# Output weights of layer 1 prepared inside the recurrence, and four operand groups instead of six

## The chip, the cores and the metric

The kernel runs on 1 core of one Trainium2 chip. The metric is the device time of one execution in microseconds (us). Three runs of the kernel before took 3316.65, 3322.71 and 3327.7 us; the median is 3322.71.

## What is computed

A decoder trunk of two residual layers on 2048 tokens of width 1024, in float32. Layer 0 mixes with pooling and convolution, layer 1 with a chunked gated DeltaNet; each is followed by a mixture of experts. Cut to what matters here, layer 1 is:

```python
u = h @ w_in                                   # q, k, v, z and the gates
state, o = scan(step, state0, chunks)          # the delta rule, in order of time
#   v_new = u_i - w_i @ state
#   o_i   = qg_i @ state + a_i @ v_new
#   state = state * d_i + kd_i^T @ v_new
y = (o * rsqrt(mean(o*o) + EPS) * onorm_g * silu(z)) @ w_out
x = x + g_m * y                                # g_m: one gate per output column, from the conditioning c
hn = rmsnorm(x, norm_ffn) * (1 + sc_f) + sh_f
x = x + g_f * hierarchical_moe(hn)             # router logits, top 1 group, top 2 experts
```

## The kernel before, in words

**Stages.** `trunk` runs layer 0, its experts (`moe(0)`), the mixer of layer 1 (`mixer1`: `dn_project`, then `dn_chain`), the output projection with the router (`out_phase(1)`), the experts (`moe(1)`) and a final norm. A tile framework orders each engine's instructions ahead of the run from dependencies, program order as priority, and a cost model; each engine then works through its list in order and waits at semaphores. A tile's space in SBUF is given to a later tile once the earlier one's last reader is done.

**The recurrence (`dn_chain`).** The 2048 tokens are 16 blocks of 128; 8 heads are two groups of four (`hg`). For a block and a group, `R(bl, hg)` has three steps: `dv = VP - KE S` (four matmuls, DVE, L1463), `vt = tt dv` (four matmuls, ACT, L1471), then the output `po = QG S + A vt` (L1476, L1477) and the new state `S = etot*S + KDD vt` (POOL makes `sd` at L1468, DVE adds at L1481). The five operands A, KE, QG, KDD, VP of a group lie in one tile `stin` of 1280 KB, loaded by `load` (L1388). There are six such tiles, in two pools of three. `load_n` (L1395 to L1403) brings the small pieces from which `M(bl, hg)` builds the block's inverse `tt` (POOL spreads at L1356; L1425 to L1452 on PE, DVE and ACT). `M` runs one to two blocks ahead of `R`. `tail` (L1496, L189, L1502, L1507) scales the outputs of the block before, `O` (L1514, L1517) transposes them, `store` (L1523) writes them to the scratch tensor `yT`. All these transfers are issued on SP's queue, in one order. Blocks 0 to 4 also carry `dn_invert(1, 1)`, DVE work on the tile `xblk` (L1321, L1322) whose result (L1323, L1327) `load_n(8)` and later ones read.

**The projection (`out_phase`, l = 1).** Its code begins by loading `w_out1`, eight pieces of 512 KB (L509), into the tiles that the experts use later for their weights (`raw`); then `load_y(0)` and `load_y(1)` (L485, L489: `yr` from `yT`, `zr` from `zT`; L490 multiplies them). Each weight piece is split into a rounded part `woh` (ACT, L237) and a remainder `wol` (DVE, L238); `yr` likewise into `yh`, `yl`. Three rows, `gm` (the gate), `ga` and `sh`, are spread over the partitions by `row_bcast` (PE L199, ACT L200). Then 16 tiles of 128 tokens: `project(t)` does 48 matmuls (L536) into a PSUM tile `po` and the epilogue

```python
nc.vector.tensor_mul(h, ps, gm)        # L540
nc.vector.tensor_add(x, h, x)          # L541
```

followed by the norm (L544, L189, L546, L547); `logits(t - 1)` transposes (L564), multiplies by the router's weights (L571) and, per group of tiles, calls `route`. After the last tile `rank_experts` gives the order of the experts, from which `moe(1)` takes the addresses of its loads.

## Time and profile before

| | us |
|---|---|
| median of three runs | 3322.71 |
| the profiled execution | 3314.97 |
| its span in the trace | 3313.2 |
| PE busy (matmuls) | 2908.4 (88%) |
| DVE busy | 2443.9 (74%) |
| ACT busy | 1495.1 (45%) |
| POOL busy | 1022.7 (31%) |

The span has six stages; times are us from its start. The stages that the change touches are the recurrence (2219 to 2475) and the projection with the router (2475 to 2760). A line such as `2490.76 1.23 DVE L490 TENSOR_TENSOR yr<-yr,zr ... [1.38 <-DMA zr<-zT]` means: begun at 2490.76, 1.23 us long, on DVE, line 490, writes yr from yr and zr, and DVE sat idle for 1.38 us before it until a DMA had brought zr. PEclk is TensorE's granted clock as a share of full speed. Matmul ends are modelled, so the distance between starts is their pace.

### The profile page before, as it was taken

To read this page: it belongs to the slowest core of one execution; us is meant where nothing else is said; L and a number is where in the kernel's file an instruction comes from. 1 tells how busy PE (TensorE), PEld (TensorE's weight loads), DVE (VectorE), ACT (ScalarE), POOL (GpSimd) and SP (SyncE) were. 2 spreads that over 40 slices of the span, in tenths; PEclk is the share of its full clock that TensorE was granted. 3 is DMA by queue.
4 is the path that set the end of the run, shared out by engine and by line. 5 is a ranking of instruction groups with operands and counts; after the bars stand their busy time and mean duration, and the time that the engine had idled before them with its cause. 6 is when DMAs were issued, how large, how long until landed. Compare 5 with 4: busy or idle time off the path is not lost. (4 is left out here: it accounts for less than half of the span.)

```text
span 3313.2 us, 41885 instructions
## 1 busy us (share of the span) xinstructions
PE 2908.4 (88%) x14192; PEld 2313.6 (70%) x14192; DVE 2443.9 (74%) x3805; ACT 1495.1 (45%) x2560; POOL 1022.7 (31%) x877
## 2 busy tenths in 40 slices
PE   4979878787999997999989999988988996999991
PEld 3756666566777774888867877777987765777770
DVE  4998999757878875777876786858445556888783
ACT  6135233216656546443444433444772214666552
POOL 0142323333443431322212131235530212434431
PEclk9989999898999998999999999998999997999996
DMA  6225233638999854545352343457957437989876
GB/s 222 85 73 209 83 132 127 216 121 303 309 281 298 268 169 160 171 153 191 136 174 83 104 144 106 144 148 223 268 195 227 153 121 253 308 279 297 264 232 217
DMA packets 384984, 633.37 MB, mean 191 GB/s; under 512 B 111232, under 2 KB 245504, under 8 KB 384768
## 3 DMA queue, kind: packets, MB, share of 16 engines
q1 hardware_dynamic: 355904, 563.38, 49.9%
q0 software_dynamic: 28864, 67.30, 8.7%
q8 instruction: 113, 1.85, 0.2%
q14 instruction: 103, 0.84, 0.1%
HBM read 484.46 MB, written 175.44 MB: 199 GB/s over the span
## 5 line engine op out<-in xcount | busy, mean ns | idle before, releaser
L260 PE MATMUL pm<-hh,wh 128*128 128x512 f32 x1408 | 565.9, 402 | 0.8 <-ACT wh L237 0.7
L262 PE MATMUL pm<-hh,wl 128*128 128x512 f32 x1408 | 556.5, 396 | 3.6 <-DVE wl L238 3.6
L261 PE MATMUL pm<-hl,wh 128*128 128x512 f32 x1408 | 555.4, 395 | 4.2 <-DVE hl L233 4.2
L238 DVE TENSOR_TENSOR wl<-wr,wh 128x1024 fp32r<-128x1024 f32 x384 | 452.2, 1218 | 40.7 <-ACT wh L237 37.3
L237 ACT ACTIVATE wh<-wr 128x1024 fp32r<-128x1024 f32 x384 | 399.5, 1057 | 134.7 <-PE py L851 56.8
L838 POOL DMA_INDIRECT acc<-ys,ixs x102 | 263.5, 2584 | 435.3 <-DVE wl L238 149.6
L261 PEld LDWEIGHTS pm<-hl,wh 128*128 128x128 f32 x1408 | 269.2, 191 | 63.4 <-DVE hl L233 4.6
L260 PEld LDWEIGHTS pm<-hh,wh 128*128 128x128 f32 x1408 | 269.1, 191 | 62.5 <-issue 4.6
L262 PEld LDWEIGHTS pm<-hh,wl 128*128 128x128 f32 x1408 | 268.6, 191 | 62.9 <-DVE wl L238 5.7
L817 PE MATMUL pu<-wh,xt 128*128 128x512 f32 x656 | 268.8, 410 | 0.5 <-ACT xt L237 0.5
L818 PE MATMUL pu<-wl,xt 128*128 128x512 f32 x656 | 261.3, 398 | 0.0
L819 PE MATMUL pu<-wh,xt 128*128 128x512 f32 x656 | 260.3, 397 | 0.0
L238 DVE TENSOR_TENSOR wl<-wraw,wh 128x1024 fp32r<-128x1024 f32 x88 | 110.9, 1261 | 155.4 <-ACT wh L237 155.2
L286 DVE SCALAR_TENSOR_TENSOR acc<-cin,wfir,acc 128x512 f32<-128x512 f32 (+1 forms) x320 | 214.7, 727 | 0.1
L536 PE MATMUL po<-woh,yh 128*128 128x512 f32 x512 | 172.4, 413 | 30.6 <-ACT yh L237 22.1
L237 ACT ACTIVATE wh<-wraw 128x1024 fp32r<-128x1024 f32 x88 | 93.2, 1059 | 227.4 <-PE pm L261 227.2
L1220 DVE SCALAR_TENSOR_TENSOR dacc<-ub,cols,dacc 128x1024 f32<-128x1024 f32 x144 | 186.8, 1297 | 2.8
L536 PE MATMUL po<-wol,yh 128*128 128x512 f32 x512 | 166.6, 405 | 0.0
L536 PE MATMUL po<-woh,yl 128*128 128x512 f32 x512 | 165.5, 402 | 0.3 <-DVE yl L238 0.3
L795 POOL DMA_INDIRECT xg<-hn,ixs x102 | 112.4, 1102 | 162.6 <-PE tp L805 87.3
L189 POOL TENSOR_TENSOR rs<-rs1t,expo 128x1 f32<-128x1 f32 x48 | 28.3, 589 | 381.1 <-DVE rs1t L187 339.6
L819 PEld LDWEIGHTS pu<-wh,xt 128*128 128x128 f32 x656 | 124.1, 189 | 30.8 <-DVE xt L238 0.5
(377 smaller groups left out, 6362.2 us busy)
## 6 DMA issues: line engine op xcount, KB each, us to landing
wr<-in_w_up_dram SPq DMA_DIRECT2D x256, 512.0 KB, 7.6
wr<-in_w_down_dram SPq DMA_DIRECT2D x128, 512.0 KB, 7.0
modw<-in_modwT_dram SPq DMA_DIRECT2D x96, 512.0 KB, 5.1
wraw<-in_w_in_dram SPq DMA_DIRECT2D x88, 512.0 KB, 3.6
stin<-stg SPq DMA_DIRECT2D x32, 1280.0 KB, 10.4
yr<-yT SPq DMA_DIRECT2D x32, 512.0 KB, 4.7
acc<-xo SPq DMA_DIRECT2D x32, 512.0 KB, 4.1
hn<-ho SPq DMA_DIRECT2D x32, 512.0 KB, 3.2
```

The source lines that it names most:

```text
L237: a = nc.scalar.activation(h, x, AF.Copy) if eng == "act" else nc.vector.tensor_copy(h, x)
L238: return a, nc.vector.tensor_sub(l, x, h.bitcast(F32))
L260: nc.tensor.matmul(ps, wh[:, k], hh[:, k], start=k == 0, stop=False)
L261: nc.tensor.matmul(ps, wh[:, k], hl[:, k], start=False, stop=False)
L262: nc.tensor.matmul(ps, wl[:, k], hh[:, k], start=False, stop=k == KD - 1)
L286: self.tap = nc.vector.scalar_tensor_tensor(o, x, w, i, op0=ALU.mult, op1=ALU.add)
L536: nc.tensor.matmul(ps[:, ns], a[:, k], b[:, ns], start=k == 0 and i == 0, stop=k == KD - 1 and i == 2)
L817: nc.tensor.matmul(ps, xh[:, k], uh, start=k == 0, stop=False)
L818: nc.tensor.matmul(ps, xh[:, k], ul, start=False, stop=False)
L819: nc.tensor.matmul(ps, xl[:, k], uh, start=False, stop=k == KD - 1)
L838: st = nc.gpsimd.indirect_dma_start(out=self.acc, out_offset=bass.IndirectOffsetOnAxis(ap=ix[:, 0:1], axis=0), in_=ys, in_offset=None, bou ...
L1220: nc.vector.scalar_tensor_tensor(acc, ub[:, i:i + 1024], self.col("dn_conv", si * 4 + i), acc, op0=ALU.mult, op1=ALU.add)
```

## The change

Five edits, all in layer 1:

1. **Weights.** A generator `weights()` in `dn_chain` fetches `w_out1` piece by piece, multiplies each by the gate row `gm`, splits it, and leaves the result in a new pool `cwo` (64 KB per partition for the two parts, 4 KB for `gm`) on the right side of SBUF. It is stepped twice in each of blocks 6 to 15. `out_phase(1)` takes the finished tiles.
2. **Epilogue.** `out_phase(1)` adds `ps` to `x` directly; the multiplication by `gm` is gone there.
3. **Operand groups.** `stin` has four tiles in one pool. `load(bl + 2, hg)` stands behind the last step of `R(bl, hg)` and no longer at the beginning of block `bl`. The small pieces have four sets instead of five; `load_n(bl + 3)` stands at the beginning of block `bl`, where `load_n(bl + 4)` stood in its middle.
4. **In place.** `dv` overwrites VP, `vt` overwrites KE, POOL writes its product into the new state's tile, the scaled outputs overwrite `ob`.
5. **Order and space.** `out_phase(1)` runs inside `mixer1`; `moe(1)` opens its own `raw` pool; the last stores of `dn_project` (zs, kg, vp) are tied behind `load_n(2)` instead of behind the loads of block 2.

```diff
-            wh = wa.tile([P, KD, D], F32R, name="woh")
-            wl = [p.tile([P, KD // 2, D], F32R, name="wol") for p in (wa, wb)]
-            if raw:
-                stage = [raw.tile([P, D], F32, name="wr") for _ in range(KD)]
-            else:
+            if l == 0:
...
+            if l == 0:
+                for k in range(KD):
+                    self.prep = self.split(wh[:, k], wl[k // 4][:, k % 4], stage[k])
+                ga, sh, wr = self.out_rows(l, wp, pt)
+            else:
+                wh, wl = self.outw
+                ga, sh, wr = self.out_rows(l, ep("wo", 1), pt)
...
-                nc.vector.tensor_mul(h, ps, gm)
-                nc.vector.tensor_add(x, h, x)
+                if l == 0:
+                    nc.vector.tensor_mul(h, ps, gm)
+                    nc.vector.tensor_add(x, h, x)
+                else:
+                    nc.vector.tensor_add(x, ps, x)
...
+            wo = ctx.enter_context(tc.tile_pool(name="cwo", bufs=1, side="right", reuse_waits="tile"))
+            self.dn_chain(yT, wo)
+            for _ in self.out_phase(1, yT, xsrc):
+                pass
...
-            ld = ep("cld", 5)
+            ld = ep("cld", 4)
-            sp = [ep(f"cst{i}", 3) for i in range(2)]
+            sp = ep("cst", 4)
...
-                    dv = t4(f"dv{hg}", 1)
-                    self.dv = nc.vector.tensor_sub(dv, VP, mm(KE, S, "pr", pr))
-                else:
-                    dv = VP
+                    self.dv = nc.vector.tensor_sub(VP, VP, mm(KE, S, "pr", pr))
+                if bl < 15:
+                    S2 = t4(f"S{hg}")
                 if 0 < bl < 15:
-                    sd = t4(f"sd{hg}", 1)
-                    nc.gpsimd.tensor_mul(sd, S, self.etot[:, hg * 4:hg * 4 + 4, bl:bl + 1].to_broadcast([P, 4, P]))
+                    nc.gpsimd.tensor_mul(S2, S, self.etot[:, hg * 4:hg * 4 + 4, bl:bl + 1].to_broadcast([P, 4, P]))
                 yield
-                vt = t4(f"vt{hg}")
-                self.vt = nc.scalar.activation(vt, mm(tt, dv, "pr", pr), AF.Copy)
+                vt = KE
+                self.vt = nc.scalar.activation(vt, mm(tt, VP, "pr", pr), AF.Copy)
...
-                        nc.vector.tensor_add(S2, sd, mm(KDD, vt, "pr", pr))
+                        nc.vector.tensor_add(S2, S2, mm(KDD, vt, "pr", pr))
...
+            def weights():
+                wh = wo.tile([P, KD, D], F32R, name="woh")
+                wl = wo.tile([P, KD, D], F32R, name="wol")
+                stage = []
+                def fetch(k):
+                    if k < KD:
+                        w = iv.tile([P, D], F32, name="wraw", tag=("xblk", "sqk")[k % 2], bufs=1)
+                        nc.sync.dma_start(w, ins["w_out1"][k])
+                        stage.append(w)
+                fetch(0)
+                fetch(1)
+                gm = wo.tile([P, D], F32, name="gm", tag="sh")
+                self.row_bcast(pm, self.mod[:, 64:72], gm, "mm")
+                yield
+                for k in range(KD):
+                    w = stage[k]
+                    nc.vector.tensor_mul(w, w, gm)
+                    yield
+                    self.split(wh[:, k], wl[:, k], w)
+                    fetch(k + 2)
+                    yield
+                self.outw = wh, (wl[:, :4], wl[:, 4:])
...
-                    if bl + 2 < 16:
-                        last = both(bl + 2)[-1]
-                    if bl == 0:
                         for sd in (kg, zs, vp):
                             behind(sd, last)
+                    if bl == 6:
+                        assert next(self.inv, None) is None
+                        prep = weights()
+                    if bl + 3 < 16:
+                        load_n(bl + 3)
...
-                    if bl + 4 < 16:
-                        load_n(bl + 4)
                     if bl > 1:
                         store(bl - 2)
...
                     run(r[0])
+                    if bl + 2 < 16:
+                        load(bl + 2, 0)
                     run(m[0])
                     next(self.inv, None)
+                    if bl > 5:
+                        run(prep)
                     run(r[1])
+                    if bl + 2 < 16:
+                        load(bl + 2, 1)
                     run(m[1])
...
                     if bl:
                         O(bl - 1, 1)
+                    if bl > 5:
+                        run(prep)
```

## Rows read from the trace of the kernel before

**Rows 1.** PE's own order from the last matmuls of the recurrence to the first of the projection: start, us, engine, line, out<-in, count, and in brackets PE's idle time before and what ended it.

```profile
2465.90 0.39 PE L1477 MATMUL po<-vt,stin 128*128 128x128 f32 x2
2466.13 1.04 PE L1514 MATMUL mm<-ident,on 128*128 128x128 f32 x8
2472.29 2.53 PE L1514 MATMUL mm<-ident,on 128*128 128x128 f32 x8 [5.12 <-ACT on L1507]
2475.66 1.97 PE L199 MATMUL tp<-ident,mod 128*128 128x128 f32 x8 [0.84 <-DVE ot L1517]
...
2493.13 1.22 PE L536 MATMUL po<-woh,yh 128*128 128x512 f32 x2 [11.30 <-ACT yh L237]
...
```

**Rows 2.** SP's queue around the same place (issue times of transfers).

```profile
2460.43 0.50 SPq L522 DMA_DIRECT2D wr<-in_w_r_dram  x1
2471.89 1.29 SPq L509 DMA_DIRECT2D wr<-in_w_out_dram  x3
2475.63 0.38 SPq L1523 DMA_DIRECT2D yT<-ot  x1
2476.06 3.82 SPq L509 DMA_DIRECT2D wr<-in_w_out_dram  x5
2479.98 0.38 SPq L485 DMA_DIRECT2D yr<-yT  x1
2480.45 2.96 SPq L489 DMA_DIRECT2D zr<-zT  x1
```

**Rows 3.** DVE and ACT around the same place.

```profile
2459.19 0.38 ACT L1452 ACTIVATE tt<-mm 64x256 f32<-64x256 f32 x1 [0.83 <-PE mm L1451]
2468.88 0.29 ACT L1489 ACTIVATE osq<-ob 128x128 bf16<-128x128 f32 x1
2471.83 2.45 ACT L1507 ACTIVATE on<-ob,fac 128x128 f32<-128x128 f32 x8 [2.57 <-DVE fac L1502]
...
2490.76 1.23 DVE L490 TENSOR_TENSOR yr<-yr,zr 128x1024 f32<-128x1024 f32 x1 [1.38 <-DMA zr<-zT]
2492.02 1.06 ACT L237 ACTIVATE yh<-yr 128x1024 fp32r<-128x1024 f32 x1 [3.90 <-DVE yr L490]
```

**Rows 4.** Busy time by stretch: us of the span, length, busy us of PE, PEld, DVE, ACT and POOL with instruction counts, granted clock, DMA share, GB/s. The first three are the handover and the projection, the others stretches of the recurrence.

```profile
2475.00:2493.00 18.00, 5.07 (x24) 3.81 (x24) 11.37 (x10) 12.19 (x15) 0.00 (x0) 0.59 1.10 352
2493.00:2505.00 12.00, 11.87 (x45) 9.71 (x46) 4.90 (x4) 1.13 (x2) 0.00 (x0) 0.86 1.01 293
2505.00:2731.00 226.00, 214.74 (x983) 162.87 (x982) 127.75 (x222) 50.56 (x82) 35.12 (x39) 0.97 0.49 157
...
2283.00:2303.00 20.00, 14.30 (x108) 12.30 (x105) 20.00 (x31) 8.22 (x31) 10.85 (x8) 0.97 0.51 166
2371.00:2386.00 15.00, 14.32 (x126) 14.06 (x125) 7.14 (x20) 10.10 (x38) 9.30 (x10) 1.00 0.88 252
```

**Rows 5.** Durations (ns, least, median, most) of the weight splits, and the time from issue to landing of two tiles' transfers: first zr, then stin.

```profile
L237 ACT ACTIVATE woh<-wr x8: 1047/1056/1057, 2475.8 to 2487.1; 128x1024 fp32r<-128x1024 f32 x8
L238 DVE TENSOR_TENSOR wol<-wr,woh x8: 1219/1225/1226, 2476.9 to 2488.1; 128x1024 fp32r<-128x1024 f32 x8
...
DMA to landing us min/median/max: 4.2/5.7/7.3
DMA to landing us min/median/max: 6.1/10.4/16.5
```

**Rows 6.** One steady block, in order: PE at its beginning and at the next one's, the last KDD matmuls of the two groups, and DVE before the state of the second group.

```profile
2371.18 0.83 PE L1379 MATMUL pr<-S,stin 128*128 128x128 f32 x6
2378.07 1.06 PE L1379 MATMUL pr<-vt,stin 128*128 128x128 f32 x8
2380.97 1.06 PE L1379 MATMUL pr<-vt,stin 128*128 128x128 f32 x8
2385.84 0.39 PE L1379 MATMUL pr<-S,stin 128*128 128x128 f32 x2
2382.06 0.69 DVE L1481 TENSOR_TENSOR S<-sd,pr 128x512 f32<-128x512 f32 x1 [2.01 <-PE pr L1379]
```

**Rows 7.** A small DVE operation beside a POOL spread of block 4, that spread, and the same operation at the end of block 8.

```profile
2287.32 1.25 DVE L1497 TENSOR_TENSOR oss<-oss,fo 128x8 f32<-128x8 f32 x1
2286.27 2.26 POOL L1356 TENSOR_TENSOR tt<-xd,m 128x512 f32<-128x512 f32 x1
2370.14 0.17 DVE L1497 TENSOR_TENSOR oss<-oss,fo 128x8 f32<-128x8 f32 x1
```

**Rows 8.** SP's queue at the beginning and at the end of the inversion, and PE at the beginning of block 6.

```profile
2232.26 5.24 SPq L1193 DMA_DIRECT2D stg<-vp  x1
2237.61 4.24 SPq L1314 DMA_DIRECT2D xblk<-ndia  x1
...
2311.75 0.33 SPq L1323 DMA_DIRECT2D xinv<-xblk  x1
2312.43 2.08 SPq L1327 DMA_DIRECT2D xsub<-xblk  x4
...
2318.49 1.82 SPq L1388 DMA_DIRECT2D stin<-stg  x2
2323.52 0.44 PE L1379 MATMUL pr<-S,stin 128*128 128x128 f32 x2
```

**Rows 9.** The last tile's epilogue on DVE.

```profile
2731.58 1.23 DVE L540 TENSOR_TENSOR ho<-po,gm 128x1024 f32<-128x1024 f32 x1 [9.28 <-PE po L536]
```

More of the change, by code (lines that the diff above doesn't have):

```diff
@@ L190, in rstd, with row_bcast @@
         return r
-    def row_bcast(self, psum, src, out):
+    def row_bcast(self, psum, src, out, tag="tp"):
         nc = self.nc
         for h in range(2):
-            p = psum.tile([P, 512], F32, name="tp")
+            p = psum.tile([P, 512], F32, name=tag)
             for j in range(4):
@@ L507, in out_phase @@
                 stage += [cv.tile([P, D], F32, name="wraw", tag="acc", bufs=NACC) for _ in range(2)]
-            for k in range(KD):
-                nc.sync.dma_start(stage[k], ins[f"w_out{l}"][k])
+                for k in range(KD):
+                    nc.sync.dma_start(stage[k], ins[f"w_out{l}"][k])
             yin = [load_y(t) for t in range(2)]
             yin[0] = split_y(0, yin[0])
-            for k in range(KD):
-                self.prep = self.split(wh[:, k], wl[k // 4][:, k % 4], stage[k])
-            if gm is None:
-                gm = wp.tile([P, D], F32, name="gm")
-                self.row_bcast(pt, self.mod[:, l * 48 + 16:l * 48 + 24], gm)
-            ga = wp.tile([P, D], F32, name="ga")
-            self.row_bcast(pt, self.gain[l, 1], ga)
-            sh = wp.tile([P, D], F32, name="sh")
-            self.row_bcast(pt, self.mod[:, l * 48 + 24:l * 48 + 32], sh)
-            wr = wp.tile([P, KD, 36], F32, name="wr")
-            nc.sync.dma_start(wr, ins["w_r"][l])
+            if l == 0:
+                for k in range(KD):
[4 more added lines that the diff above has]
+                ga, sh, wr = self.out_rows(l, ep("wo", 1), pt)
             mcum = rt.tile([P, NT + 1, NE], BF16, name="mcum", bufs=1)
@@ L589, in out_phase, with out_rows @@
             self.rank_experts(l, mcum[:, NT], rt, pr)
+    def out_rows(self, l, pool, psum, tag="tp"):
+        ga = pool.tile([P, D], F32, name="ga")
+        self.row_bcast(psum, self.gain[l, 1], ga, tag)
+        sh = pool.tile([P, D], F32, name="sh")
+        self.row_bcast(psum, self.mod[:, l * 48 + 24:l * 48 + 32], sh, tag)
+        wr = pool.tile([P, KD, 36], F32, name="wr")
+        self.nc.sync.dma_start(wr, self.ins["w_r"][l])
+        return ga, sh, wr
     def rank_experts(self, l, mc, rt, pr):
@@ L748, in route_setup, with moe @@
             self.lists.append(lst)
-    def moe(self, l, raw=None):
+    def moe(self, l):
         tc, nc, ins = self.tc, self.nc, self.ins
@@ L1385, in load @@
                 half, b = divmod(bl, 8)
-                s = sp[(bl * 2 + hg) // 3 % 2].tile([P, 4, 5, P], F32, name="stin")
+                s = sp.tile([P, 4, 5, P], F32, name="stin")
                 loaded[bl, hg] = s
@@ L1402, in load_n @@
                 for i in range(2):
-                    last = nc.sync.dma_start(nds[bl % 5][i * 64:(i + 1) * 64, :, i], self.stg[half][b][:64, i::2, 0, 64:])
+                    last = nc.sync.dma_start(nds[bl % 4][i * 64:(i + 1) * 64, :, i], self.stg[half][b][:64, i::2, 0, 64:])
                 blocks[bl] = (x, xd, no)
@@ L1528, in run @@
                     next(g, None)
+            def weights():
[12 more added lines that the diff above has]
+                yield
+                for k in range(KD):
+                    w = stage[k]
[5 more added lines that the diff above has]
+                self.outw = wh, (wl[:, :4], wl[:, 4:])
             if True:
@@ L1666, in trunk @@
         T.moe(0)
-        T.mixer1(yT[1])
-        with tc.tile_pool(name="mraw1", bufs=RAW, reuse_waits="tile") as raw:
-            for _ in T.out_phase(1, yT[1], lambda t: T.x2[t * P:(t + 1) * P], None, raw):
-                pass
-            T.moe(1, raw)
+        T.mixer1(yT[1], lambda t: T.x2[t * P:(t + 1) * P])
+        T.moe(1)
         T.final(out)
```

33 lines of the change are left out of this document (16 added, 17 removed).

## The prediction

> **What bounds the kernel now.** I read the busy time by stretch first, then the order of each engine where a stretch is poor. Three things are to be seen. In the steady second part of the recurrence PE works 14.3 of 15 us, DVE 7.1, ACT 10.1 and POOL 9.3, and the DMA engines are 0.88 busy [rows 4]; a block begins every 14.66 us (2371.18 to 2385.84) [rows 6]. So PE sets the pace there, and DMA is not far behind. In the projection PE works 214.7 of 226 us [rows 4]: what begins earlier ends earlier. Between the two lies a hole. PE's own order shows the recurrence's last matmul at 2465.9, ending at 2466.3, then only transposes, and the first projection matmul at 2493.13, after 11.30 us of idle time [rows 1]: a handover of 26.8 us. What ends last in it is read backwards: the matmul waits for yh (ACT, 2492.02), that for yr*zr (DVE, 2490.76), that for the transfer of zr [rows 3]. zr was issued at 2480.45, behind eight weight pieces that SP could issue only from 2471.89 on [rows 2], and in this stretch the DMA engines move 352 GB/s and are full (share 1.10) [rows 4]. The handover is bound by 4.2 MB of weights standing ahead of the first tile.
>
> **The change, part by part.** The sum goes against the profiled execution, 3315.0 us (span 3313.2 and 1.8 around it); the median of the three runs is 7.7 above it.
>
> *Handover.* The weights, their splits and the gate row leave it. Late next is yr and zr of tile 0. Their space is that of the recurrence's small constant tiles, which the last `M` reads; it ends at 2459.19+0.38 [rows 3]. I expect SP to issue them then, ahead of the last two stores: w_r, which also stands behind those stores in the code, went out at 2460.43 [rows 2]. With zr's median of 5.7 us [rows 5] both are in at about 2466. The product (1.23) fits DVE's idle time, but ACT works through squares until 2468.88+0.29; its split (1.06) [rows 3] then ends at 2470.2. PE can begin 3.9 us after the recurrence. Not hidden: the transposes of block 15's output and of two rows instead of three, 8 and 16; eight take 1.04 us at full clock (2466.13) and 1.97 to 2.53 in the cold stretch [rows 1], so 3.1 to 7 us, of which some 2 fit the 3.9. The handover becomes about 8 us, a gain of 19. Bounds: 21 if nearly all the transposes fit; if SP keeps to the order of the code, yr and zr go out behind the last store, at 2476.0 and 2476.5 [rows 2], land at 2482.2, and with 1.23 and 1.06 PE begins at 2484.5, a gain of 8.7.
>
> *Clock.* In the handover the granted clock is 0.59, which is 1.2 GHz for most of it, and in the first 12 us of the projection 0.86 [rows 4]: the missing 0.14 of 12 us is 1.7 us. With 4 us of idle time in place of 11.30 some of it goes. Between 0 and 1.7 I take 1.
>
> *PE work put into the recurrence.* The gate row's eight transposes cost 1.04 us [rows 1] where PE sets the pace: +1.0, and nothing to speak of on either side.
>
> *DVE and ACT work put into the recurrence.* Blocks 6 to 15 get eight products and eight remainders on DVE, 16 times 1.22 = 19.6 us, and eight roundings on ACT, 8 times 1.06 = 8.5 us [rows 5]. (The product's duration is that of the remainder, the same shape with two SBUF sources.) In each of some nine blocks that is 2.4 us on a DVE with 7.5 us free and 1.1 on an ACT with 4.5 free [rows 4]. Cover: free time comes in pieces, the largest 2.01 us before the second group's state [rows 6]; a piece of 1.22 us that begins too late delays a dv or S behind it in DVE's order, and PE's next matmuls wait for that. From below 0 (all in gaps); from above all of 19.6. The nearest row that shows DVE overfull is block 4: DVE 20.0 of 20 us, and the block takes 20 us instead of 14.66 [rows 4], 5.4 us more with some 12 us of inversion work. At 9.6 of 14.66 DVE is far from that, so I take 0.4 a block, +3.6.
>
> A row speaks against this. Beside a POOL spread of 2.26 us a DVE operation on 8 columns took 1.25 us, which takes 0.17 when alone [rows 7]. The Trainium skill, SBUF — State Buffer, section "Who interferes with whom", states that a DVE instruction with two SBUF inputs and a GpSimd instruction that reads SBUF exclude each other, and whichever began first blocks the other for its whole length. By that rule all 16 new operations are of the exposed kind, while most DVE work of a steady block has a PSUM input; it is the rival B below. The rows agree that the wait exists; how often it would fall on the path they don't show.
>
> *DMA work put into the recurrence.* Eight pieces of 512 KB at the handover's 352 GB/s are 1.5 us each; a steady block leaves 0.12 of 15 us, 1.8 us [rows 4]. It just fits; the handover's gain already counts its absence there.
>
> *Four groups instead of six.* A load now waits until the last KDD matmuls of the same group two blocks earlier. In the steady block these end 8.0 and 10.9 us after its beginning (2379.1 and 2382.0) [rows 6], and the first use is 29.3 us after it; landing takes 10.4 us in the median and 16.5 at most [rows 5], so the load is in 2 to 11 us early. Queued behind it on SP are the next small pieces and a store, which need a block less. Cost 0. The tight place is block 6. In the code its loads now stand behind the inversion's store, which SP could issue only at 2311.75 [rows 8]; before, they stood ahead of it. Behind that store and its scatter they go out at 2314.5 and land, at 6.1 to 16.5 us [rows 5], between 2320.6 and 2331, against a first use at 2323.5 [rows 8]: 0 to 7.5 us. Against that, kg, vp and zs go out before block 2's loads, so the load that begins the inversion, at 2237.61 behind 5.24 us of vp's issue [rows 8], can go out earlier, and up to 5 us of the crowded blocks 1 to 5 may come back. I take 0 for the two.
>
> *In place.* The same instructions on other addresses: 0, with a gain or loss under 0.5 us in the pace, since each overwritten operand has had its last reader by then.
>
> *Epilogue.* DVE loses 16 products of 1.23 us, but PE, not DVE, bounds the projection; only the last tile's stands on the path [rows 9]: -1.2. That `moe(1)` no longer inherits its weight tiles costs nothing: its loads need addresses from the ranking, which ends later than the last reader of that space.
>
> Sum: -19 - 1 + 1 + 3.6 + 0 - 1.2 = -16.6. Against the profiled execution 3298; against the median 3322.7 - 16.6 = **3306**.
>
> **Rivals.** *A, the handover stays long.* SP issues yr and zr behind the last store, or the PSUM bank of the first `po` is one that block 15's transposes still hold until 2475.6 (the row transposes at 2475.66 waited for just that) [rows 1]. The gain is 8.7 instead of 19; with the other terms -6, 3316. For it: SP's order in the rows is mostly the code's; against it: w_r.
>
> *B, the recurrence slows through the port shared by DVE and POOL, and the kernel becomes slower.* Place: blocks 6 to 15, each new DVE operation blocked by a spread or state product of POOL, or blocking one. Price: up to 1.1 us of waiting (1.25 less 0.17) [rows 7] on top of 1.22, 2.3 us each and 37 us for 16 if all stood on the path. That in place of the 3.6 gives 3306 + 33 = 3339. It decides from 20 us on (3306 + 16.7 = 3323, no gain left), which is 55% of the price on the path. Against it: POOL is idle for 5.7 of 15 us, and the two groups of heads cover for each other.
>
> *C, the four groups starve.* The loads of block 6 come 7.5 us late, and the gate of blocks 7 and 8 passes on half of it: +11, 3317. For it: a DMA share of 0.88; against it: 11 us of reserve at the median landing.
>
> *D, it does what it says and more:* the inversion's earlier start gives 5 us, and the transposes all fit: 3297.
>
> **How the numbers follow.** Forecast with D 0.60 (its own range 3294 to 3312), A 0.18, C 0.10, B 0.12. A measurement of this kernel can tell a change from none from about 0.3% on, 10 us: 3313 and 3333. Faster by more: the forecast and a part of A, 0.64. Within: most of A and C and the milder B, 0.25. Slower by more: B from 30 us on, 0.09, and A together with C or with a milder B, 0.02. The range takes in D's side and runs past A and C into B: 3292 to 3327.
>
> **What would show it.** Right: the first projection matmul 6 to 10 us after the last recurrence matmul, no weight transfer in that stretch, yr issued before the last store; blocks 7 to 14 at 15.0 to 15.3 us each; stin never ending a PE wait; the last epilogue with one DVE operation less. Wrong: blocks at 16 us or more with DVE operations of 1.22 us stretched to 2 or more beside spreads (B); PE waiting for stin in block 6 (C); zr still ending the handover's wait behind the last store (A).

## The result, and the profile after

| | before | after |
|---|---|---|
| median of five runs, us | 3322.71 | 3293.99 |
| lowest and highest, us | 3312.78, 3327.7 | 3289.09, 3303.5 |
| span of the profiled execution, us | 3313.2 | 3289.6 |

The medians differ by 28.7 us; the ratio after to before over all runs is 0.993, with a 95% interval of 0.9915 to 0.9946, which is 23 us faster, or 18 to 28. A second comparison of the two on one chip, at the end of the experiments, gave 0.9933 (0.9917 to 0.9948). The prediction was 3306, with 16.6 us of gain. The profiled spans differ by 23.6 us, and by stage this is where they went:

| stage, us | forecast | before | after | difference | after, second profile |
|---|---|---|---|---|---|
| last two splits of the projection's operands (ACT, `kqh`) to block 7 | 0 | 146.3 | 147.1 | +0.8 | 146.5 |
| block 7 to the recurrence's end | +4.6 | 124.2 | 130.1 | +5.9 | 130.2 |
| handover | -19 | 26.8 | 10.4 | -16.4 | 10.1 |
| first projection matmul to tile 0's epilogue (L540) | -1 | 13.2 | 12.6 | -0.6 | 12.7 |
| tile 0's epilogue to tile 15's | 0 | 225.2 | 214.2 | **-11.0** | 213.7 |
| tile 15's epilogue to the end | -1.2 | 581.6 | 579.8 | -1.8 | 579.5 |

(Block 7 begins where the first `dv` or `stin` difference of that block starts on DVE, 2342.11 and 2342.44; L540 of the first and the last tile start at 2506.33 and 2731.58 before, 2495.54 and 2709.75 after. What is missing to 23.6 lies ahead of the first row.) Five of the six are near the forecast. The fifth was not forecast at all, and it is nearly half of the gain.

The handover of the kernel after, from the timeline (start, us, engine, line, out<-in, count, and in brackets the idle time before and what ended it; here and below the rows are picked, and others stand between them):

```profile
2465.86 0.46 SPq L487 DMA_DIRECT2D yr<-yT  x1
2466.41 1.28 SPq L491 DMA_DIRECT2D zr<-zT  x1
2472.16 0.39 PE L1487 MATMUL po<-stin 128*128 128x128 f32 x2
2474.46 0.36 SPq L1530 DMA_DIRECT2D yT<-ot  x1
2474.67 1.23 DVE L492 TENSOR_TENSOR yr<-yr,zr 128x1024 f32<-128x1024 f32 x1 [0.24 <-DMA zr<-zT]
2475.93 1.06 ACT L237 ACTIVATE yh<-yr 128x1024 fp32r<-128x1024 f32 x1 [0.41 <-DVE yr L492]
2478.80 2.53 PE L1521 MATMUL mm<-ident,ob 128*128 128x128 f32 x8 [5.38 <-ACT ob L1515]
2481.12 2.07 PE L199 MATMUL tp<-ident,gain 128*128 128x128 f32 x8
2482.94 0.48 PE L532 MATMUL po<-woh,yh 128*128 128x512 f32 x1
```

It answers to [rows 1 to 3]. SP issues `yr` and `zr` before the last stores, as forecast, in place of eight weight pieces. The landing of `zr` (8.3 us after its issue, against the 5.7 that I took) makes the operand ready at 2477.0. The matmul then starts 5.9 us later, since block 15's transposes and the rows' stand ahead of it in PE's order: rival A's second half.

The busy time by stretch, with the columns of [rows 4] (PE, PEld, DVE, ACT, POOL, granted clock, DMA share, GB/s): block 8, a later block, the handover, the projection's first 12 us, and the projection.

```profile
2356.00:2371.00 15.00, 12.44 (x84) 11.92 (x83) 9.77 (x19) 8.67 (x23) 7.89 (x7) 0.77 0.91 267
2401.00:2416.00 15.00, 14.30 (x123) 13.79 (x122) 9.63 (x22) 11.21 (x40) 8.98 (x9) 1.00 0.89 272
2475.00:2483.00 8.00, 4.20 (x17) 3.03 (x17) 6.06 (x10) 5.57 (x15) 1.63 (x1) 0.57 0.86 243
2483.00:2495.00 12.00, 11.98 (x57) 9.62 (x56) 2.70 (x3) 1.79 (x3) 0.00 (x0) 1.00 0.92 267
2495.00:2709.00 214.00, 211.00 (x981) 159.77 (x980) 111.96 (x206) 48.97 (x82) 33.20 (x39) 1.00 0.52 165
```

A steady block has 2.5 us more of DVE (9.63 against 7.14) and 1.1 more of ACT, what was counted for it. In the projection the clock is 1.00, where it was 0.97, and PE is idle for 3 us, where it was 11.3. So PE alone did not bound the projection before: 11 us of waits, and stretches of half clock, lay in it, and my view of 214.7 busy of 226 passed over them.

### The profile page after: what moved, and what is told of

Read it like the earlier page. It is cut to its first block, busy times and chain, and to the rows that moved or that the text cites. A ratio compares the mean times of both kernels' runs of the same rounds, so it can differ in the third digit from the quotient of the medians.

```text
span 3289.6 us, 41913 instructions
## 1 busy us (share of the span) xinstructions
PE 2900.5 (88%) x14192; PEld 2309.4 (70%) x14192; DVE 2435.8 (74%) x3797; ACT 1493.0 (45%) x2559; POOL 1019.7 (31%) x877
## 5 line engine op out<-in xcount | busy, mean ns | idle before, releaser
L238 DVE TENSOR_TENSOR wl<-wr,wh 128x1024 fp32r<-128x1024 f32 x384 | 452.3, 1219 | 40.7 <-ACT wh L237 37.2
L828 PEld LDWEIGHTS pu<-wh,xt 128*128 128x128 f32 x656 | 124.2, 189 | 30.6 <-DVE xt L238 0.4
L826 PEld LDWEIGHTS pu<-wh,xt 128*128 128x128 f32 x656 | 124.5, 190 | 28.8 <-ACT xt L237 1.5
```

The source lines that it names most:

```text
L238: return a, nc.vector.tensor_sub(l, x, h.bitcast(F32))
L826: nc.tensor.matmul(ps, xh[:, k], uh, start=k == 0, stop=False)
L828: nc.tensor.matmul(ps, xl[:, k], uh, start=False, stop=k == KD - 1)
```

## Where the projection lost eleven microseconds

Two places carry it, behind the first two routes (the intervals between the epilogues of tiles 5 to 7 and 9 to 11 shrank by 11.9 us in all). In the kernel before, tile 5 (timeline, the second route group's first tile but one):

```profile
2574.63 1.09 POOL L711 DMA_INDIRECT lst<-pay,sl  x1 [12.37 <-DVE sl L709]
...
2579.02 0.15 DVE L187 TENSOR_SCALAR rs1t<-ss 128x1 f32<-128x1 f32 x1 [1.22 <-ACT ho L544]
2585.29 0.96 POOL L711 DMA_INDIRECT lst<-pay,sl  x1 [0.31 <-issue]
2586.27 0.58 POOL L189 TENSOR_TENSOR rs<-rs1t,expo 128x1 f32<-128x1 f32 x1
2586.89 1.28 DVE L546 SCALAR_TENSOR_TENSOR ho<-xo,rs,ga 128x1024 f32<-128x1024 f32 x1 [7.72 <-POOL rs L189]
2588.09 1.22 DVE L490 TENSOR_TENSOR yr<-yr,zr 128x1024 f32<-128x1024 f32 x1
2589.23 1.22 DVE L547 TENSOR_TENSOR ho<-ho,sh 128x1024 f32<-128x1024 f32 x1
2590.59 1.94 PE L564 MATMUL tp<-ident,ho 128*128 128x128 f32 x8 [4.78 <-DVE ho L547]
```

with the busy time of these 20 us (columns of [rows 4]):

```profile
2575.00:2595.00 20.00, 15.22 (x62) 11.43 (x61) 9.92 (x11) 5.22 (x9) 9.69 (x9) 0.84 0.42 129
```

and the same place after:

```profile
2564.02 1.09 POOL L720 DMA_INDIRECT lst<-pay,sl  x1 [13.63 <-DVE sl L718]
...
2567.79 0.15 DVE L187 TENSOR_SCALAR rs1t<-ss 128x1 f32<-128x1 f32 x1 [0.33 <-ACT ho L543]
2574.62 0.58 POOL L189 TENSOR_TENSOR rs<-rs1t,expo 128x1 f32<-128x1 f32 x1
2575.24 1.29 DVE L545 SCALAR_TENSOR_TENSOR ho<-xo,rs,ga 128x1024 f32<-128x1024 f32 x1 [7.30 <-POOL rs L189]
2576.56 1.23 DVE L546 TENSOR_TENSOR ho<-ho,sh 128x1024 f32<-128x1024 f32 x1
2577.93 1.06 PE L563 MATMUL tp<-ident,ho 128*128 128x128 f32 x8 [0.80 <-DVE ho L546]
```

After each route POOL issues eight list transfers, most of them 1.26 us apart. `rs`, which takes 0.58 us and for which the whole epilogue waits, stands behind them in both kernels: DVE waits for it 7.72 and 7.30 us. What differs is the slack. Counted from the first list transfer, PE was through with the next tile's matmuls after 11.2 us before (2590.59 - 4.78 - 2574.63) and 13.1 after; `ho` was ready after 16.0 and 13.9. The first I put down to a routing that ends earlier on a DVE with less to do; no run shows that alone. The second has two halves. DVE's order no longer puts the next tile's `yr*zr` between the last two steps, 1.0 us; and the row of transfers itself is 1.0 us shorter (11.64 to 10.60 us from the first one to `rs`): in the kernel before its second transfer took 2.64 us, beside DVE's remainder and the sum L541, after the change the longest took 1.57. Each wait of 4.8 us also cost the clock: the eight transposes behind it took 1.94 us, after the change 1.06, and from 2575 to 2595 and from 2640 to 2660 the granted clock was 0.84. Four experiments take this apart.

**The product put back.** The changed kernel with the gate in the epilogue again.

```diff
...
-                    nc.vector.tensor_add(x, ps, x)
+                nc.vector.tensor_mul(h, ps, gm if l == 0 else self.gm1)
+                nc.vector.tensor_add(x, h, x)
...
-                    nc.vector.tensor_mul(w, w, gm)
```

> The changed kernel with the product of the gate back in layer 1's epilogue (the weights are split ungated; the gate row stays). Theory: the 11.0 us that the projection lost (225.25 to 214.21 us from the first tile's L540 to the last tile's) come from the product alone: with it in the epilogue's chain, rs of the second tile after a route is asked for later, behind the list transfers on POOL, and PE waits 4 to 5 us for ho at two places. Then the projection is 224 to 226 us again, the waits of PE for ho are 4 to 5 us, and the recurrence, which loses eight of the sixteen new DVE operations, ends 1 to 3 us earlier: span 3297 to 3301. Rival: the projection is shorter because PE comes into it warm and the other weight work and its transfers are gone: then it stays at 213 to 216 us, the waits at 1 us or less, and the span at 3286 to 3290.

Measured: the projection 226.67 us, the waits 4.48 and 4.45, span 3308.2. The product put back costs 12.5 us, so the theory holds for the projection; the recurrence went the other way (below).

**The product taken out of the kernel before.**

```diff
-                nc.vector.tensor_mul(h, ps, gm)
-                nc.vector.tensor_add(x, h, x)
+                if l == 0:
+                    nc.vector.tensor_mul(h, ps, gm)
+                    nc.vector.tensor_add(x, h, x)
+                else:
+                    nc.vector.tensor_add(x, ps, x)
```

> The kernel before with one edit: layer 1's epilogue adds the projection to x without the gate. It leaves the gate of layer 1's output out altogether; the handover with its eight weight pieces stays. Theory (the product alone): the projection falls from 225.25 to 213 to 217 us, the handover stays at 26 to 27 us, span 3301 to 3304. The prediction's step (PE bounds the projection, only the last tile's product counts): 224 us, span 3312. Rival (warm entry, no weight work): 224 to 225 us.

Measured: the projection 213.40 us, the waits 1.09 and 1.06, the handover still 26.94. The prediction's step and the warm entry are both out: the product alone makes 11.9 us. (The span says nothing here, 3431.1 us: without the gate the router sends the tokens elsewhere, and the experts have other work.)

**`rs` ahead of the list transfers, in the kernel before.** The eight transfers are kept back for one tile.

```diff
...
                 project(t)
+                if self.late:
+                    with tc.issue_after(self.rs.ins):
+                        for f in self.late:
+                            f()
+                    self.late = []
...
-            for i in range(m):
-                st = nc.gpsimd.indirect_dma_start(
+            def issue(sl=sl, k=k):
+                for i in range(m):
+                    st = nc.gpsimd.indirect_dma_start(
...
+            if l and t0 + m < NT - 1:
+                self.late.append(issue)
```

> The kernel before with the eight list transfers of a route issued on POOL behind rs of the next tile but one instead of ahead of it; nothing else changes. Theory: the 4.78 and 4.75 us that PE waits for ho at tiles 5 and 9 are rs standing behind these transfers (11.6 us from first to last); with rs ahead both waits fall under 1 us, the matmuls at half the granted clock after them go, and the projection falls from 225.25 to 213 to 216 us: span 3301 to 3305, the same gain as taking the product out. Rival: what is late is the DVE chain itself (product, sum, two more), and rs is only the last to arrive: the waits stay at 3 us or more, projection 221 or more. A second rival: the transfers, now later, stand ahead of rs of the following tile and move the wait there: 222 to 225.

Measured: the projection 209.68 us and no wait for `ho` at tiles 5 and 9 any more, with the gate still in the epilogue and the weights still in the handover; span 3296.6, where the kernel before beside it on the same chip had 3311.4. From its timeline:

```profile
2579.95 0.54 POOL L189 TENSOR_TENSOR rs<-rs1t,expo 128x1 f32<-128x1 f32 x1 [17.05 <-DVE rs1t L187]
...
2580.53 1.28 DVE L546 SCALAR_TENSOR_TENSOR ho<-xo,rs,ga 128x1024 f32<-128x1024 f32 x1 [0.72 <-POOL rs L189]
2580.70 2.08 POOL L718 DMA_INDIRECT lst<-pay,sl  x1 [0.20 <-issue]
...
2586.29 1.03 PE L564 MATMUL tp<-ident,ho 128*128 128x128 f32 x8
```

So the stall is `rs` behind the transfers: with `rs` ahead of them it is gone, product or not, and removing the product had won a part of it by the way. This edit of the order is worth more in the projection (15.6 us) than all that the change did there.

**The same in the changed kernel.**

> The changed kernel with the list transfers on POOL behind rs of the next tile but one, as in the experiment on the kernel before (projection 225.25 to 209.68 us there). Theory: what the product's removal won was only its share of the same stall; with rs ahead the projection is the same with or without the product: 208.5 to 210.5 us instead of 214.21, span 3285 to 3286. Rival: with the waits at 0.80 and 0.78 us nothing but these is left: 212.5 to 213.5.

Measured: 212.28 us, 0.2 below the rival's range and far from the theory's. No wait for `ho` is left in it, yet it is 2.6 us slower than the kernel before with the same edit. The difference is not in a wait: a pair of matmuls begins 0.466 to 0.469 us after the one before (median of a tile), where the kernel before has 0.467 in the odd tiles and 0.454 in the even ones.

**Where the operand lies.** In the kernel before, the even tiles' `yh` and `yl` lie in SBUF between the two halves of the low weights, the odd ones' above them; in the changed kernel both lie below the weights. In the kernel before, the odd tiles' were moved next to the even ones':

```diff
-            ys = [ep("yo0", 1), None]
+            ys = [ep("yo0", 1), ep("yo1", 1)]
             wb = ep("wob", 1)
-            ys[1] = ep("yo1", 1)
```

> The kernel before with the buffers of the odd tiles' operand moved next to those of the even tiles, between the two halves of the low weights (both layers); nothing else changes. In the kernel before a pair of projection matmuls of an even tile begins every 0.454 us and of an odd tile every 0.467, in both layers; the even tiles' operand lies between the weights' halves, the odd tiles' above them; in the changed kernel it lies below the weights for both, and both take 0.467. Theory (the place of the operand): now both 0.453 to 0.456, some 0.3 us less for each odd tile, 2 to 2.5 us a layer. Rival (it belongs to odd tiles by their place in the loop, to the transfers that run beside them, or to a parity of another buffer): odd tiles stay at 0.466 to 0.467. A second rival: both become slow, since the operand must lie in one place alone.

Measured: 0.453 or 0.454 in every odd tile, in both layers, as in the even ones (of these four, three of them in layer 0, have 0.457 to 0.467; layer 0 has such tiles in the kernel before too); projection 223.3 us instead of 225.2. An odd tile (tile 3) in the timelines of the kernel before and of the one with this edit:

```profile
2536.34 0.63 PE L536 MATMUL po<-woh,yh 128*128 128x512 f32 x2
2536.81 0.63 PE L536 MATMUL po<-wol,yh 128*128 128x512 f32 x2
```

and with the edit:

```profile
2547.07 0.61 PE L535 MATMUL po<-wol,yh 128*128 128x512 f32 x2
2547.52 0.62 PE L535 MATMUL po<-woh,yl 128*128 128x512 f32 x2
```

The change thus gave back an estimated 2.4 us (8 even tiles of 24 pairs, 0.0125 each) by where it put its buffers; between the two kernels with the edit of the order it is 2.6 us.

## The recurrence: the same work in another place

The steady block went from 14.66 to 14.95 us, +0.29 where I had 0.4. But of the 5.9 us that the recurrence lost, 4.8 lie in blocks 7 and 8 (29.9 us before, 34.7 after). DVE and PE in block 8 of the changed kernel:

```profile
2356.60 1.22 DVE L1556 TENSOR_TENSOR wraw<-wraw,gm 128x1024 f32<-128x1024 f32 x1
2358.41 1.22 DVE L1556 TENSOR_TENSOR wraw<-wraw,gm 128x1024 f32<-128x1024 f32 x1
2359.55 1.23 DVE L238 TENSOR_TENSOR wol<-wraw,woh 128x1024 fp32r<-128x1024 f32 x1
2360.90 0.17 DVE L187 TENSOR_SCALAR orst<-oss 128x8 f32<-128x8 f32 x1
2361.11 1.22 DVE L238 TENSOR_TENSOR wol<-wraw,woh 128x1024 fp32r<-128x1024 f32 x1
2361.14 2.04 PE L1441 MATMUL mm<-xo,w 128*128 128x256 f32 x4 [2.56 <-DVE orst L187]
2362.97 1.92 PE L1391 MATMUL pr<-S,stin 128*128 128x128 f32 x8
```

SP issued the first two pieces together (2340.46, two transfers in 1.73 us), and DVE's order has their work together: two products and two remainders nearly in a row. The small operations that PE needs come behind three of them, PE waits 2.56 us, and after that its eight matmuls take 1.92 us instead of 1.06: the granted clock of 2362 to 2370 is 0.69.

**One block later.** Two more steps ahead of the first product.

```diff
                 self.row_bcast(pm, self.mod[:, 64:72], gm, "mm")
-                yield
+                for _ in range(3):
+                    yield
```

> The changed kernel with the products and splits of the weights traced two steps (one block) later. Theory: in block 8 two products and two remainders (4.9 us) stood in one row on DVE ahead of the small operations that PE waited for, since the first piece landed a block later than its product stood in the order; this one block took 19.3 us instead of 14.95 and PE fell to the lower clock in it. One block later the pieces come one by one: no block over 15.3 us from block 8 on, recurrence 3.5 to 4.5 us shorter, span 3285 to 3286. Rival: the pieces land late whatever their place, and the pile moves to another block: one block of 17 us or more stays, span 3289 to 3290.

Measured: blocks 7 and 8 take 31.1 us, block 7 to the end 126.9 instead of 130.1, span 3286.5. The pieces come one by one, and 3.2 us return; blocks 8 and 9 still take 15.7 and 15.4, so the bound of 15.3 was missed. Of the 3.2, the clock is a good part: in three kernels of this study whose code is that of the changed one up to there (other banks, the rows earlier, and the list transfers behind `rs`), the pile is the same, the clock stayed at 1.00, the two blocks took 32.4, and block 7 to the end 127.8.

**Half of the work, and slower.** In the kernel with the product back in the epilogue DVE has eight operations less in the recurrence, and I had expected 1 to 3 us less. Its block took 15.55 us, and from block 7 to the end 133.5. Its steady block, in the timeline:

```profile
2409.95 1.21 DVE L238 TENSOR_TENSOR wol<-wraw,woh 128x1024 fp32r<-128x1024 f32 x1
2410.13 2.35 POOL L1365 TENSOR_TENSOR xo<-xh,m 128x256 f32<-128x256 f32 x2
2411.09 1.54 DVE L1443 COPY tl<-tt 64x256 f32<-64x256 f32 x2
2412.04 0.41 PE L1447 MATMUL mm<-ident,tl 128*128 128x128 f32 x2 [1.04 <-DVE tl L1443]
```

Here is rival B's mechanism. The remainder begins 0.18 us ahead of POOL's spreads `xo`, which take 2.35 us where 1.41 to 1.47 is usual; the `tl` copies behind take 1.54 instead of 0.78. The first of these is what the Trainium skill, SBUF — State Buffer, section "Who interferes with whom", states (a DVE instruction with two SBUF inputs and a GpSimd one that reads SBUF exclude each other for the whole length of the one that began first), and the trace agrees, with 0.9 us a collision (the first `xo` takes 1.62 us instead of 0.73). The copies have one SBUF input; by the trace they wait too, since each ends 0.15 us behind the end of the spread that ran when it began.

**The remainder in DVE's largest gap**, in that kernel.

```diff
-                    self.split(wh[:, k], wl[:, k], w)
+                    with tc.issue_after(self.dv.ins):
+                        self.split(wh[:, k], wl[:, k], w)
```

> The kernel with the product back in the epilogue, with its remainders (L238) queued on DVE behind the second group's difference, that is in DVE's largest idle piece (3.56 us ahead of the state). Theory (place, not load): its blocks took 15.53 us, against 14.95 in the changed kernel with twice the DVE work, because the remainder stood beside a POOL spread; that spread took 2.35 us instead of 1.41 to 1.47, the two tl copies behind it 1.54 instead of 0.78, and PE waited 1.37 us for them. In the gap: spread and copies back at 1.4 to 1.5 and 0.8, PE's waits for tl under 0.4, a block 14.65 to 14.95 us. Rival (the amount of work on DVE and ACT, or the in-place operands): 15.4 to 15.6. A second rival: in the gap the remainder meets the spreads tt and na and makes the state late: a block over 15.1, with PE waiting for S.

Measured: 15.87 us a block, 135.1 from block 7 to the end. My theory fell: the `xo` spreads are back at 1.40, as it says, but the block is longer still. The copies now meet spreads by themselves, with no remainder near, and PE waits 0.82 and 0.86 us for them (timeline of this kernel):

```profile
2418.40 0.70 DVE L1443 COPY tl<-tt 64x256 f32<-64x256 f32 x1 [0.93 <-ACT tt L1440]
2418.92 2.58 POOL L1365 TENSOR_TENSOR tt<-xd,m 128x512 f32<-128x512 f32 x2
2419.25 0.41 PE L1447 MATMUL mm<-ident,tl 128*128 128x128 f32 x2 [0.82 <-DVE tl L1443]
2419.32 1.05 DVE L1443 COPY tl<-tt 64x256 f32<-64x256 f32 x1 [0.22 <-ACT tt L1440]
2420.52 0.41 PE L1447 MATMUL mm<-ident,tl 128*128 128x128 f32 x2 [0.86 <-DVE tl L1443]
```

What the two kernels with the longer blocks share is PE's own order: in both, the transposes of `tl` stand ahead of the second group's eight `pr<-S`, so PE has nothing to do while ACT and DVE make `tl`; in the changed one those eight and eight `pr<-stin,tt` stand in between. That this order is the cause is read from the rows; no run changed it alone, and so no run shows that the collision of the remainder made the block of the first of the two longer.

**Both in the gap, in the changed kernel** (with the weights one block later).

> The changed kernel with the weights one block later and with products and remainders queued on DVE behind the second group's difference. Theory: the 0.29 us that a block of the changed kernel takes above 14.66 stems from the remainder standing ahead of the tl copies that PE waits for (0.28 and 0.42 us); in the gap a block takes 14.65 to 14.8, and the recurrence ends 1 to 2 us earlier than with the later weights alone: span 3284 to 3286. Rival: the 0.29 belongs to the product or to PE's own order and stays: 14.95. A second rival: product, rounding and remainder now press on the state: 15.2 or more.

Measured: 14.84 us a block, 126.9 from block 7 to the end, as without the gap. Halfway between theory and rival, and worth nothing in sum. In each block the remainder now meets the `tt` spreads, which take 3.56 us instead of 2.49 (1.07 more), and nobody waits for them: the same collision, off the path.

## The handover: an earlier start that ends no earlier

**The rows ahead of block 15's tail.**

```diff
+                self.outr = self.out_rows(1, wo, pm, "mm")
                 for _ in tail(15):
...
-                ga, sh, wr = self.out_rows(l, ep("wo", 1), pt)
+                ga, sh, wr = self.outr
```

> The changed kernel with the two rows ga and sh (and w_r) made at the end of the recurrence, ahead of block 15's tail, with the recurrence's PSUM. Theory: in the handover the projection's operand is ready at 2477.0 and the first matmul is issued at 2482.94, since block 15's eight transposes (2478.80) and the rows' stand ahead of it in PE's order; the rows' sixteen fit PE's idle 5.38 us before. Handover 10.39 to 8.0 to 8.8 us, span 3287 to 3288. Rival: what holds the first matmul is the PSUM bank that block 15's transposes hold until their copies on DVE are through (2482.1): the handover stays at 9.8 to 10.4 us.

Measured: 9.33 us, between the two; the rows fill PE's wait, and then it waits 0.47 us for `yh` itself. From the recurrence's end to tile 0's epilogue it is 22.6 us instead of 23.0.

**Other PSUM banks for the projection.**

```diff
...
+            else:
+                pt = ep("pto", 2, space=PSUM)
+                pr = ep("pro", 1, space=PSUM)
+                ep("pgap", 1, space=PSUM).tile([P, 512], F32, name="gap")
+                po = ep("pso", 2, space=PSUM)
```

> The changed kernel with the projection's two PSUM tiles moved from banks 2 to 5 to banks 4 to 7 in layer 1, away from the four banks of block 15's transposes. Theory (the bank half of rival A): the operand was ready at 2477.0 and the first matmul was issued at 2482.94 only because its bank was one that block 15's transposes hold until DVE has copied them; with other banks the projection starts first and the transposes run between its matmuls: handover 10.39 to 4.5 to 6 us; the transposes' 3 us move into the projection's first tile, so from the recurrence's end to the first tile's L540 23.0 becomes 19.5 to 21.5, span 3285 to 3288. Rival: what holds the matmul is the order alone, by readiness (block 15's output is estimated ready first) or the landing of zr: handover 9.5 to 10.4, sum 22.5 to 23.5.

Measured: the first matmul 4.2 us after the recurrence. So it was the bank that kept it back; the bank half of rival A was right. But tile 0's epilogue comes 22.8 us after the recurrence's end instead of 23.0. From its timeline:

```profile
2483.79 0.74 PE L538 MATMUL po<-woh,yh 128*128 128x512 f32 x2 [3.29 <-ACT yh L237]
2485.63 0.47 PE L1527 MATMUL mm<-ident,ob 128*128 128x128 f32 x1 [1.10 <-ACT ob L1521]
2489.96 1.05 PE L538 MATMUL po<-wol,yh 128*128 128x512 f32 x2
```

The transposes wait for ACT between the matmuls, and a pair of matmuls takes 1.05 us, the length at half clock, until 2491 and later, where in the changed kernel all pairs have 0.63. The 6 us of earlier start go into these waits (3.29 and 1.10 us) and into 6 us at 1.2 GHz (granted clock 0.50 from 2485 to 2491). (Its span, 3299.1, is the beginning of the recurrence, which is told next.)

**Three edits together, and the changed kernel again.** The weights later, the list transfers behind `rs`, and the operands moved up in SBUF, to where the even tiles' were in the kernel before.

> The changed kernel with three edits: the weights one block later, the list transfers behind rs of the next tile but one, and the projection's operands yh and yl of layer 1 moved from below 70 KB of the partition to 116 to 132 KB, which is where they are in the even tiles of the kernel before, but not between the weights, which stay above 160 KB. By stages from the earlier runs: 3.2 us less in the recurrence (126.9 against 130.1 from block 7 to its end) and 1.5 to 2 us less in the projection; and if the place in the partition alone decides the matmuls' pace, 0.454 us a pair for all tiles and 4.5 us more: projection 208 us, against the changed kernel 9 to 10 us, ratio to the kernel before 0.989 to 0.991. Rival (the operand must lie between the weights' halves): 0.467 stays, projection 212 to 213 us, 5 us against the changed kernel, ratio 0.991 to 0.993. A second rival: the buffers there belong to the recurrence's last operands and output, and the split of the first tiles waits for them: the handover grows by 5 us or more and takes the gain back.

> The changed kernel as it is, for a comparison on the same chip with the one above. If the stages' differences carry through it stands 5 to 10 us behind that one, at a ratio to the kernel before of 0.992 to 0.994; within 2 us of it, they don't. From its second profile: block 7 to the end of the recurrence 127 to 131 us (130.1 in the first profile, 127.8 in two kernels with the same code there), the start of the recurrence's blocks up to 5 us off the first profile's, since kernels with the same code there differed by as much.

Measured: ratio 0.9937 (0.9924 to 0.995) for the three edits, 0.9933 (0.9917 to 0.9948) for the changed kernel: no better, where I had expected 5 to 10 us between the two. By stages the recurrence has its 3 us (127.0) and the projection its 1.4 (212.3), with 0.467 a pair: the place in the partition alone does not make the faster pace. The handover is 15.8 us, so the second rival came, though not through the operands' split. On DVE the second tile's product stood ahead of block 15's small operations and waited for its `zr` until 2485.7. That `zr` was issued 3.2 us ahead of the recurrence's end, no later than in the changed kernel (2.9); but there these operations stand ahead of the product. So `oss` began 6.2 us behind the recurrence's end (2486.93) and not 3.3 (2475.81), and PE's transposes, and behind them the projection, waited 10.17 us and not 5.38. Of the two that were run several times, then, the three edits do not beat the changed kernel. (The list transfers behind `rs` alone, or the weights later alone, save 1.4 to 1.9 and 3.2 us by stage; each had one execution, 3284.87 and 3288.25, which the scatter told next covers.)

The two profiles also show why spans of single executions scatter. The same stretch at the beginning of the recurrence, 12 to 30 us after the last splits of the projection's operands, with the three edits (windows):

```profile
2210.60:2216.60 6.00, 3.95 (x21) 3.52 (x21) 3.19 (x8) 1.85 (x7) 4.61 (x6) 0.77 1.00 333
2216.60:2228.60 12.00, 11.74 (x46) 9.72 (x45) 2.84 (x11) 3.91 (x14) 0.00 (x0) 0.50 1.04 396
```

and in the second profile of the changed kernel:

```profile
2203.20:2209.20 6.00, 4.92 (x34) 3.88 (x32) 2.63 (x9) 2.65 (x9) 5.07 (x6) 1.00 0.95 310
2209.20:2221.20 12.00, 9.52 (x69) 8.02 (x68) 3.15 (x12) 7.01 (x24) 0.00 (x0) 1.00 1.04 396
```

Both come out of 12 us in which the granted clock was 0.51 to 0.63, and in the first six of which PE was busy for less than 0.5. In the second it is back at 2.4 GHz after that; in the first, where PE was busy 3.95 of 6 us at that place and not 4.92, it is 0.77 and then 1.2 GHz for all of the next 12. From the splits to block 1 the one takes 40.7 us, the other 34.3, and four of the fourteen profiles (39.4 to 40.9) belong to the first kind: three of the ten kernels made from the changed one and one of the four made from the kernel before. Within each of these two groups the code there is the same, so the arguments here rest on stages and not on the span of one execution.

## Why the prediction was right, and where it was not

*Handover, forecast -19, measured -16.4 (26.8 to 10.4 us).* Right in its mechanism: the weight pieces gone from SP, `yr` issued ahead of the last stores, the start limited by block 15's transposes. Two sizes were off: `zr` took 8.3 us to land and not 5.7, and of the 24 transposes less fitted the wait. The part of rival A that has SP issue `yr` late is refuted by the rows, the bank half is shown by the experiment on the banks, and the same experiment shows that the bank cost nothing in the end.

*Clock, -1.* -0.6; the first 12 us of the projection now have 1.00 where they had 0.86 [rows 4].

*PE, DVE and ACT work in the recurrence, +4.6.* +5.9 and +6.0, and +3.6 in the three kernels in which the clock held. The steady pace (+0.29 us a block, with 2.5 us more on DVE) is near the 0.4 of the forecast, but its mechanism is not shown: PE's waits in a steady block (block 11) are 0.28 and 0.42 us after, and one of 0.68 before, so the 0.29 lies in longer distances between matmuls that show no wait, and no run says whether the new work, PE's other order or the overwritten tiles make them. That this size fits is in part luck. What I had not seen is that the first two pieces would come together, four operations in one block, with a drop of the clock behind them. That block took 19.3 us, over the 16 that I had named as a sign of rival B, but its operations were not stretched (1.22 and 1.23 us). Putting the steps one block later returned 3.2 us. The landing, which that expectation names as the reason for the pile, is not shown: the longest landing of a piece was 10.1 us, so both were in by 2351.5, and DVE's order has the products at 2356.60.

*Rival B, the shared port.* Its price is right (0.9 to 1.07 us a collision, where I had up to 1.1), and that it would not decide was right too, but not for the reason that I gave, how busy POOL is. In the changed kernel's steady block the new operations meet no spread: the remainder ends at 2409.39, and the first spread begins at 2409.68. Where one does meet a spread, what counts is whether PE waits for it: with both operations in the gap it meets one in each block, at 1.07 us, and the block is not longer for it (14.84). In the kernel with half of the new work the stretched copies did stand on PE's path and a block took 0.6 us more; how much of that is the collision and how much PE's order is open.

*DMA work in the recurrence, four groups, earlier inversion: 0.* +0.8 and +0.2 up to block 7. Its parts are larger and cancel, which is luck: from the splits to block 1 it is 36.3 us instead of 32.7, from block 1 to block 2 28.2 instead of 15.1, and from there to block 7 82.6 instead of 98.5. No run took these apart. Among what PE waits for in the recurrence after there is no transfer of `stin`, so rival C did not come.

*Epilogue, -1.2.* This step failed: "PE, not DVE, bounds the projection; only the last tile's stands on the path". It was taken from one row over 226 us. The 11.3 us that PE was idle in that row, and its clock of 0.97, were not asked for their places; two waits of 4.8 us for the very chain that the change shortens stand in that stage's list of waits. The product was worth 11.9 us there (taken out of the kernel before) to 12.5 (put back into the changed one), and the operands' place took an estimated 2.4 of that back. The product acts on that chain away from the last tile: with it the list transfers, and `rs` behind them, come 1.9 us later against PE's matmuls, their row is 1.0 us longer, and DVE's order has another product between the last two steps, 1.0 us; this is the whole of the way from 4.78 us of wait to 0.80. That the sum comes later cost nothing at these places: `rs1t` was ready at 2579.17, and POOL came to `rs` at 2586.27.

*In place, 0.* No run took it alone.

So the forecast was right in sign, and the median, 3293.99, lies within its range, but 2 us from the lower end. Its sum is off by 7 us (23.6 against 16.6 by the profiled spans), with two terms a little too good, one too bad by 10 us and one unseen loss by the operands' place; that these nearly stayed inside is luck. The time is close to rival D's 3297, but neither of D's reasons came: the earlier inversion gave nothing up to block 7, and the transposes did not all fit.

## What to carry to other kernels

An engine that is 95% busy over a stage need not be the bound of the stage: divide the missing 5% into its waits, look at what each ends on, and ask what the change does to that chain, also to the order of its short links. A short instruction that many wait for, here a power of 128 numbers on POOL, should not stand behind a row of issued transfers; moving it ahead was worth 15.6 us in the projection of the kernel before, more than taking a whole product out of the epilogue. And a start that is made earlier is worth what the end behind it gains: in the handover 6 us of earlier start gained 0.2.

## What I had not expected of the hardware

The pace of the projection's matmuls of 128x512 depends on where its operands lie in SBUF: a pair every 0.454 us with the stationary operand between the halves of the weights, 0.467 with it above them (odd tiles of both layers) or below (layer 1 of the changed kernel), and the pace followed the buffer when that was moved. Which property of the place decides is open; the height in the partition alone did not (0.467 when the operand was moved there).

And the granted clock took either of two courses through the same code at the beginning of the recurrence, 1.00 or, for up to 18 us, 0.50, at 6 us of difference.
